# A planner's price of TensorE: a lower rate per column and a larger fixed part

## The chip, the cores and the metric

The kernel runs on one core of a Trainium2 chip. The metric is the device time of one execution, in microseconds (us), median over runs. A core has TensorE (PE: matmuls and transposes), VectorE (DVE), ScalarE (ACT), GpSimd (POOL) and SyncE (SP, whose queue issues all loads and stores here). Each engine takes its own instructions in the order in which the program issued them.

## What is computed

Two layers over a sequence of 512 rows of 1024 float32 values. Each layer:

```
h = rms_norm(x) * g_pre_mix
pool values | q | k | v | indexer q, k, head weights = h @ w_in           # 1024 x 2632
score  = sum over 8 heads of iw * relu(iq . ik / 8)      # 512 x 512, causal by chunks of 64
keys of a row = the 128 largest scores                   # top-k
B = softmax(q . k / 8 over those keys) @ v               # 8 heads of 64
A = averages over windows of 2, 4, 8, 16 rows, minus the row, @ w_pool, * pool_scale
x = x + rms_norm(concat(A, B) @ w_out) * g_post_mix
x = x + rms_norm(relu(rms_norm(x) * g_pre_ffn @ w_ff1)^2 @ w_ff2) * g_post_ffn   # 4096 wide
```

## The kernel before

The 512 rows are four tiles t of 128 rows; a contraction over 1024 is eight chunks kc of 128. Float32 values are split into two float32r parts (a rounded one and the rest), and each product is three matmuls (`mm3`) into one PSUM bank. `A` in SBUF holds the two parts of the normalized rows, transposed.

**Weights** (`WeightStream`) come in chunks of 128 rows by 512 columns (584 for the indexer), 400 in all. SP loads two chunks into a tile `wraw`, of which there are two; `_split` (L445) then writes a tile `ws` from a ring of eight: a cast (`copy`, L536: ScalarE or VectorE) and a subtraction (`tt`, L531: VectorE or GpSimd). `ws.done()` starts the next split when a chunk was last used.

**Stages of a layer.** Indexer projection for t = 0 to 3 (tiles `pi`, 292 columns), with ropes, transposes (`tr`), 8 logits per tile (`lg`), relu and the sum `sc`; then the projections q, k, v (tiles `pg`, 512 columns). `select(t)` (L806) finds the 128 largest scores of a row: 16 rounds on VectorE of MAX8 (`m8`) and MATCH_REPLACE8 (`bias`). `attention(t)` (L871), in the order 2, 3, 0, 1, makes per head logits (`s`), exponentials, a scaling, transposes (`pt`, split into `pT`) and products with v (`po`). The pooling mixer (tiles `pool`, `mx`, `dh`) stands behind attention(2) in the program. The output projection takes tiles 2 and 3, then 0 and 1; each ends in `post_norm` (L686) and `pre_norm`, which scales `h` and transposes it (`hT`) into `A`. The feed-forward network runs in four groups of two blocks of w_ff1 (`pf`, `pg`; relu `fr`, square, split into `f`) and 1024 rows of w_ff2, summed in SBUF (`facc`).

**The planner decides the order.** The program's calls are not issued at once. `_Recorder` (L348) notes each with its price, and `Planner.record` finds what it depends on. `Planner.issue` (L191) makes a list schedule: `sweep` (L227) goes forward through time and gives each engine, of the instructions it could start, the one that must start soonest, then goes backward to find how late each may end (`late`, L222); of 40 such rounds, each with the times of the one before, the shortest is issued. Where an instruction has two possible engines, `sooner` (L258) decides whether one should leave it to the other:

```python
in_time, other = mine <= late[i] - self.SPARE, done <= late[i] - self.SPARE
if in_time and w != 0:
    continue
if other and v != 0 and not (in_time and w != 0):
    return True
```

SPARE is 4000 ns (L95): an instruction that the second engine (v != 0) would end 4 us before its latest time goes there; otherwise it goes where it ends sooner. The second engine is VectorE for casts and relus, GpSimd for subtractions and additions in SBUF, ScalarE for scalings. Prices are in `cost` (L356), waits between engines in LATENCY (L87). A price under 60 ns on TensorE counts as short, and a longer instruction behind a short one starts 54 ns later in the plan (L313 to L315).

Of the kernel before, what the change touches and what calls it, by code (L numbers as in the profile page):

```python
# [18 lines left out]
P = 128  # L19
# [62 lines left out]
class Planner:  # L82
    """Takes the instructions down in program order, finds what each depends on from the tiles that it
    reads and writes, and issues them in the order of a list schedule over the engines: of the
    instructions that an engine could start, the one with the longest chain of work behind it."""
# [55 lines left out]
    def either(self, *ways):  # L141
        """One instruction that several engines can take: each way makes one call."""
        self.collected = []
        for way in ways:
            way()
        found, self.collected = self.collected, None
        self.record([(e, c, f) for e, c, f, _, _ in found], found[0][3], found[0][4])
# [43 lines left out]
    def issue(self):  # L191
        """Sweeps forward and backward over the program in turn, each sweep taking its order of
        preference from the times of the one before, and issues in the order of the best. The first
        order is that of the longest chains behind, with a little noise to part equal ones."""
# [32 lines left out]
    def sweep(self, key, pred, succ, late, fixed=None):  # L227
        """A list schedule. With ``fixed``, the ways are given and time runs backward."""
# [29 lines left out]
        def sooner(t, i, w):  # L258
            """Whether another engine should take instruction i."""
# [76 lines left out]
class _Recorder:  # L336
# [19 lines left out]
    def cost(self, method, args, kw, out, reads):  # L356
        def free(ap):
            return math.prod(c for _, c in list(ap.ap)[1:])
# [6 lines left out]
        if self.name == "pe":  # L365
            if method == "transpose":
                return 56 if args[1].dtype == F32R else 109
            return max(n / 2.4 + 2.5, 107 if free(args[1]) > 64 else 56)
# [16 lines left out]
class WeightStream:  # L385
    """Chunks of weights in the order of their use: loaded, split into two float32r parts, and held
    in a ring until their last use."""
# [21 lines left out]
    def add_paired(self, src, r0, nrows, c0, ncols):  # L409
        """Chunks of 256 rows: rows r and r + 128 side by side."""  # L410
# [59 lines left out]
def hymba_trunk(ctx: ExitStack, tc: tile.TileContext, x, positions, g_pre_mix, w_in, w_pool,  # L470
# [60 lines left out]
    def tt(out, a, b, op, first="dve"):  # L531
        """an elementwise instruction on SBUF, on VectorE or GpSimd"""
        ways = [lambda: dve.tensor_tensor(out, a, b, op=op), lambda: pool.tensor_tensor(out, a, b, op=op)]
        planner.either(*(ways if first == "dve" else ways[:1]))

    def copy(out, a):  # L536
        """a copy, on ScalarE or VectorE"""
        planner.either(lambda: act.activation(out, a, AF.Copy), lambda: dve.tensor_copy(out, a))

    def scaled(out, a, by):  # L540
        """rows times a scalar of each, on VectorE or ScalarE"""
# [109 lines left out]
    def square(out, a, total):  # L651
        """total = the sum of (a / 32) ** 2 along the row: a half's part of the row's mean square"""
        act.activation(out, a, AF.Square, scale=1.0 / 32.0, accum_out=total)

    def rstd_of(parts):
        """parts: [P, 2], the two halves' parts of the row's mean square"""
# [5 lines left out]
    def pre_norm(t, gain):  # L662
        """A[:, :, :, tile t] = the two parts of (RMSNorm(x[t]) * gain) transposed."""
# [22 lines left out]
    def post_norm(t, halves, gain, in_sbuf=False):  # L686
        """x[t] += RMSNorm(halves) * gain"""
# [21 lines left out]
    def rope(row, t, heads):  # L709
        """in place on the first 16 of each head's 64 columns."""  # L710
# [8 lines left out]
    def heads_stacked(dst_hl, row, heads):  # L719
        """dst[128, heads, 2, 64]: the two parts of each head side by side."""  # L720
# [4 lines left out]
    def heads_doubled(dst, row, heads):  # L725
        """dst[128, 2, heads, 2, 64]: either part of each head, twice side by side."""
# [4 lines left out]
    def transposed(dst, srcs):  # L731
        """dst [128, n, 128] <- transposes of n blocks of [128, 128] in float32r."""
# [14 lines left out]
    for l in range(DEPTH):  # L747
# [11 lines left out]
        # indexer projection, logits and scores  # L759
# [103 lines left out]
        # attention  # L863
# [118 lines left out]
        # feed-forward  # L982
# [102 lines left out]
```

## Time and profile before

| | |
|---|---|
| time, median of 3 runs | 1223.35 us (1222.40, 1223.35, 1226.63) |
| profiled execution: first to last instruction (span); its own time beside it is not given | 1222.7 us |
| instructions | 16265, of them 5880 matmuls |
| busy: TensorE, VectorE, GpSimd, ScalarE | 1178.5, 777.1, 668.5, 358.5 us |
| mean granted clock of TensorE | 0.996 |
| read from HBM | 112.27 MB; 94 GB/s over the span with what is written |

"Busy" is the time in which an engine had an instruction under way. What ended an engine's idle time stands in brackets behind the instruction that followed, with the idle time. Stretches are in us from the span's start: attention of layer 0 60 to 240, its output projection and handover to the feed-forward network 240 to 276.9, feed-forward to 605, handover to layer 1 605 to 632, its attention 660 to 840, its feed-forward from 879.5, last matmuls 1207.8 to 1213.5.

### The profile page before, as it was taken

What the parts mean: (1) busy time and instruction counts of PE and PEld (TensorE: products, weight loads), DVE (VectorE), ACT (ScalarE), POOL (GpSimd) and SP (SyncE); (2) the same over time, 40 slices, a digit from 0 to 9 for tenths busy, and PEclk for the clock granted to TensorE, in tenths of its full rate; (3) what the DMA queues carried; (4) which work ended last, traced back from release to release, by engine and by line L of the source; (5) the groups of instructions that cost most, each with busy time, mean ns of one, the idle gap of its engine ahead of it and who ended that gap; (6) DMA issues with size and microseconds to landing.
All of it is one profiled execution on the core that took longest, in us unless ns stands there. A gap on an engine that the chain in (4) does not pass through costs nothing.

```text
span 1222.7 us, 16265 instructions
## 1 busy us (share of the span) xinstructions
PE 1178.5 (96%) x5880; PEld 978.3 (80%) x5880; DVE 777.1 (64%) x1620; ACT 358.5 (29%) x840; POOL 668.5 (55%) x628
## 2 busy tenths in 40 slices
PE   5999999999999999999989999999999999999996
PEld 5987878788888888888887878787888888888885
DVE  8899999875216335245779999998632353343344
ACT  5444677540010000000354367675201000000011
POOL 4145331358659659558334543314785695684782
PEclk9999999999999999999999999999999999999999
DMA  7222222433332322332322222234234223323221
GB/s 242 70 56 67 69 69 88 138 105 121 106 101 69 121 86 71 119 93 90 113 70 69 69 69 69 71 104 138 86 104 121 87 83 107 104 86 104 87 87 69
DMA packets 62160, 115.41 MB, mean 94 GB/s; under 512 B 5248, under 2 KB 10368, under 8 KB 62080
## 3 DMA queue, kind: packets, MB, share of 16 engines
q1 hardware_dynamic: 62080, 114.38, 29.9%
q8 instruction: 46, 0.75, 0.3%
q14 instruction: 34, 0.28, 0.1%
HBM read 112.27 MB, written 2.10 MB: 94 GB/s over the span
## 4 chain that ended last, share of the span: by engine, by line
PE 68%; DVE 23%; issue 5%; POOL 1%; DMA 1%; ACT 0%; DVEq 0%; SPq 0%; POOLq 0%; ACTq 0%
PE pg L349 58%; DVE ws L349 4%; DVE bias L349 3%; PE pi L349 2%; DVE m L349 2%; PE pf L349 2%; DVE mx L349 2%; DVE sc L349 2%; DVE x L349 1%; DVE s L349 1%; DVE A L349 1%; DVE h L349 1%; DVE pT L349 1%; PE lg L349 1%; PE pool L349 1%
## 5 line engine op out<-in xcount | busy, mean ns | idle before, releaser
L349 POOL TENSOR_TENSOR ws<-wraw,ws 128x512 fp32r<-128x512 f32 x296 | 397.6, 1350 | 278.0 <-DVE ws L349 233.3
L349 DVE CAST ws<-wraw 128x512 fp32r<-128x512 f32 (+1 forms) x317 | 195.3, 624 | 337.1 <-PE pg L349 247.4
L349 PE MATMUL pg<-A,ws 128*128 128x512 f32 x1344 | 313.9, 395 | 0.0
L349 PEld LDWEIGHTS pg<-A,ws 128*128 128x128 f32 x1344 | 252.3, 188 | 60.0
L349 PE MATMUL pg<-ws,A 128*128 128x512 f32 x864 | 226.3, 400 | 1.9 <-DVE pn L349 1.6
L349 PE MATMUL pg<-ws,f 128*128 128x512 f32 x768 | 187.0, 394 | 0.0
L349 PEld LDWEIGHTS pg<-ws,A 128*128 128x128 f32 x864 | 156.9, 188 | 33.5 <-DVE pn L349 2.5
L349 PEld LDWEIGHTS pg<-ws,f 128*128 128x128 f32 x768 | 144.1, 188 | 33.6
L349 ACT ACTIVATE fr<-pg 128x512 f32<-128x512 f32 x49 | 27.9, 598 | 475.9 <-PE pg L349 475.1
L349 PE MATMUL pg<-ws,f1h 128*128 128x512 f32 x512 | 149.5, 394 | 0.0
L349 PEld LDWEIGHTS pg<-ws,f1h 128*128 128x128 f32 x512 | 96.1, 188 | 22.5
L349 POOL TENSOR_TENSOR rstd<-rstd,neg_half 128x1 f32<-128x1 f32 x32 | 25.9, 809 | 119.5 <-DVE rstd L349 114.9
L349 PE MATMUL pg<-ws,f1l 128*128 128x512 f32 x256 | 89.1, 393 | 0.0
L349 DVE TENSOR_TENSOR ws<-wraw,ws 128x512 fp32r<-128x512 f32 (+1 forms) x104 | 79.0, 772 | 0.9 <-ACT ws L349 0.5
L349 POOL TENSOR_TENSOR fr<-fr 128x512 f32<-128x512 f32 (+1 forms) x70 | 71.3, 1033 | 12.8 <-ACT fr L349 11.8
L349 ACT ACTIVATE s<-s,st 128x384 f32<-128x384 f32 (+3 forms) x96 | 54.0, 568 | 36.0 <-DVE st L349 32.5
L349 PE MATMUL pi<-ws,A 128*128 128x292 f32 x384 | 60.7, 305 | 2.2 <-DVE ws L349 1.8
L349 ACT ACTIVATE ws<-wraw 128x512 fp32r<-128x512 f32 (+1 forms) x83 | 51.9, 632 | 30.1 <-PE pg L349 19.8
L349 PE MATMUL pool<-A,ws 128*128 128x512 f32 x192 | 58.7, 407 | 0.0
L349 PEld LDWEIGHTS pg<-ws,f1l 128*128 128x128 f32 x256 | 48.1, 188 | 11.2
L349 PEld LDWEIGHTS pi<-ws,A 128*128 128x128 f32 x384 | 53.4, 190 | 3.7 <-DVE ws L349 2.4
L349 DVE CAST f1h<-fr 128x512 fp32r<-128x512 f32 (+1 forms) x40 | 39.2, 997 | 19.0 <-POOL fr L349 19.0
(154 smaller groups left out, 1493.7 us busy)
## 6 DMA issues: line engine op xcount, KB each, us to landing
wraw<-in_w_ff_dram SPq DMA_DIRECT2D x128, 512.0 KB, 3.7
wraw<-in_w_out_dram SPq DMA_DIRECT2D x32, 512.0 KB, 3.6
wraw<-in_w_in_dram SPq DMA_DIRECT2D x24, 512.0 KB, 3.6
wraw<-in_w_in_dram SPq DMA_DIRECT2D x8, 584.0 KB, 4.1
wraw<-in_w_in_dram SPq DMA_DIRECT2D x16, 256.0 KB, 3.0
x<-in_x_dram SPq DMA_DIRECT2D x4, 512.0 KB, 6.3
out_dram<-x SPq DMA_DIRECT2D x8, 256.0 KB, 2.0
gain<-in_g_pre_mix_dram SPq DMA_DIRECT2D x2, 512.0 KB, 4.7
```

The source lines that it names most:

```text
L349: lambda: getattr(self.real, method)(*args, **kw))
```

## The change

`cost` prices TensorE's instructions by other numbers. Nothing else of the program differs, beside comments and docstrings, which issue nothing.

```diff
         if self.name == "pe":
             if method == "transpose":
-                return 56 if args[1].dtype == F32R else 109
-            return max(n / 2.4 + 2.5, 107 if free(args[1]) > 64 else 56)
+                return 59 if args[1].dtype == F32R else 109
+            return max(4.5 + n / 2.25, 111 if free(args[1]) > 64 else 60)
```

In ns, by columns: 512 from 215.8 to 232.1; 384 from 162.5 to 175.2; 292 from 124.2 to 134.3; 256 from 109.2 to 118.3; 128 from 107 to 111; a float32r transpose from 56 to 59, still short. Weights of 64 columns or fewer do not occur. TensorE's large matmuls become 7 to 8% dearer in the plan; all other prices stay. The same work is issued in another order, and some instructions that two engines can take go to the other one.

**VectorE, layer 0, the first weights of q** (`ws_257` to `ws_261`, while the indexer's second tile `irow_201` is roped and split into `ihl`; `bias0` is the selection of tile 0). Before:

```order
L349 CAST ws_257<-wraw_127 128x512
L349 SCALAR_TENSOR_TENSOR bias0_374<-sc0_182,bias0_374 128x128
L349 CAST ihl_204<-irow_201 128x8x64
L349 TENSOR_TENSOR ws_257<-wraw_127,ws_257 128x512
L349 TENSOR_TENSOR ihl_204<-irow_201,ihl_204 128x8x64
L349 TENSOR_TENSOR ws_258<-wraw_127,ws_258 128x512
L349 TENSOR_TENSOR ws_260<-wraw_130,ws_260 128x512
L349 COPY iqS_206<-tr_208 128x512
L349 TENSOR_SCALAR bias0_374<-bias0_374 128x128
L349 CAST ws_261<-wraw_130 128x512
L349 TENSOR_TENSOR ws_261<-wraw_130,ws_261 128x512
```

Now:

```order
L349 CAST ws_257<-wraw_127 128x512
L349 SCALAR_TENSOR_TENSOR bias0_374<-sc0_182,bias0_374 128x128
L349 CAST ihl_204<-irow_201 128x8x64
L349 CAST ws_258<-wraw_127 128x512
L349 TENSOR_TENSOR ihl_204<-irow_201,ihl_204 128x8x64
L349 TENSOR_TENSOR ikh_205<-irow_201,ikh_205 128x128
L349 CAST ws_260<-wraw_130 128x512
L349 TENSOR_SCALAR bias0_374<-bias0_374 128x128
L349 COPY iqS_206<-tr_208 128x512
L349 CAST ws_261<-wraw_130 128x512
```

The four subtractions of `ws_257` to `ws_261` have left VectorE for GpSimd, and the casts of `ws_258` and `ws_260` have come to it from ScalarE; so it goes on for the weights of q, k, v, pool and the first output pass.

**VectorE, layer 1, scores of tile 3** (`sc3_1141`, summed over the heads' relus) beside the selection of tile 2 (`bias2_1216`, `m82_1217`). Before:

```order
L349 TENSOR_SCALAR sc3_1141<-relu_1143,iw_1133 128x512
L349 MAX m82_1217<-bias2_1216 128x8
L349 SCALAR_TENSOR_TENSOR sc3_1141<-relu_1145,iw_1133,sc3_1141 128x512
L349 MATCH_REPLACE bias2_1216<-m82_1217,bias2_1216 128x384
L349 SCALAR_TENSOR_TENSOR sc3_1141<-relu_1147,iw_1133,sc3_1141 128x512
L349 MAX m82_1217<-bias2_1216 128x8
L349 SCALAR_TENSOR_TENSOR sc3_1141<-relu_1149,iw_1133,sc3_1141 128x512
L349 MATCH_REPLACE bias2_1216<-m82_1217,bias2_1216 128x384
L349 SCALAR_TENSOR_TENSOR sc3_1141<-relu_1151,iw_1133,sc3_1141 128x512
```

Now:

```order
L349 TENSOR_SCALAR sc3_1141<-relu_1143,iw_1133 128x512
L349 TENSOR_SCALAR relu_1145<-lg_1144 128x512
L349 MAX m82_1217<-bias2_1216 128x8
L349 SCALAR_TENSOR_TENSOR sc3_1141<-relu_1145,iw_1133,sc3_1141 128x512
L349 MATCH_REPLACE bias2_1216<-m82_1217,bias2_1216 128x384
L349 TENSOR_SCALAR relu_1147<-lg_1146 128x512
L349 MAX m82_1217<-bias2_1216 128x8
L349 SCALAR_TENSOR_TENSOR sc3_1141<-relu_1147,iw_1133,sc3_1141 128x512
L349 MATCH_REPLACE bias2_1216<-m82_1217,bias2_1216 128x384
L349 MATCH_REPLACE bias1_1235<-m81_1236,bias1_1235 128x256
L349 MAX m82_1217<-bias2_1216 128x8
```

The relus of the logits `lg`, 128x512, have come from ScalarE to stand between the sums.

**VectorE, the last instructions of the program** (`post_norm` of tiles 1 to 3; `pg_1843` and `pg_1844` are the last PSUM banks of tiles 2 and 3). Before:

```order
L349 SCALAR_TENSOR_TENSOR x1_112<-pn_1848,rstd_1850,x1_112 128x512 x2
L349 TENSOR_TENSOR facc_1601<-pg_1843,facc_1601 128x512
L349 TENSOR_TENSOR pn_1854<-facc_1601,gain_1549 128x512
L349 TENSOR_TENSOR pn_1851<-facc_1601,gain_1549 128x512
L349 SCALAR_TENSOR_TENSOR rstd_1853<-ss2_1852 128x1
L349 TENSOR_TENSOR facc_1601<-pg_1844,facc_1601 128x512
L349 SCALAR_TENSOR_TENSOR x2_113<-pn_1851,rstd_1853,x2_113 128x512 x2
L349 SCALAR_TENSOR_TENSOR rstd_1856<-ss2_1855 128x1
L349 SCALAR_TENSOR_TENSOR x3_114<-pn_1854,rstd_1856,x3_114 128x512 x2
```

Now:

```order
L349 TENSOR_TENSOR pn_1851<-facc_1601,gain_1549 128x512
L349 SCALAR_TENSOR_TENSOR x1_112<-pn_1848,rstd_1850,x1_112 128x512
L349 SCALAR_TENSOR_TENSOR rstd_1853<-ss2_1852 128x1
L349 TENSOR_TENSOR pn_1854<-facc_1601,gain_1549 128x512
L349 SCALAR_TENSOR_TENSOR x2_113<-pn_1851,rstd_1853,x2_113 128x512
L349 TENSOR_TENSOR facc_1601<-pg_1844,facc_1601 128x512
L349 SCALAR_TENSOR_TENSOR x2_113<-pn_1851,rstd_1853,x2_113 128x512
L349 TENSOR_TENSOR pn_1854<-facc_1601,gain_1549 128x512
L349 SCALAR_TENSOR_TENSOR rstd_1856<-ss2_1855 128x1
L349 SCALAR_TENSOR_TENSOR x3_114<-pn_1854,rstd_1856,x3_114 128x512 x2
```

The accumulation of `pg_1844` has one update of `x2` and one gain product `pn_1854` ahead of it and one of each behind; the second product came from GpSimd.

## Rows read from the trace of the kernel before

**Rows 1.** the page's first part: busy us, share of the span, instructions

```profile
PE 1178.5 (96%) x5880; PEld 978.3 (80%) x5880; DVE 777.1 (64%) x1620; ACT 358.5 (29%) x840; POOL 668.5 (55%) x628
```

**Rows 2.** busy time by stretch: length, busy us and instructions, granted clock, DMA

```profile
330.00:600.00 270.00, 270.00 (x1165) 218.33 (x1164) 114.59 (x155) 18.94 (x37) 177.99 (x138) 1.00 0.30 95
60.00:240.00 180.00, 175.16 (x933) 143.71 (x932) 173.12 (x458) 107.62 (x260) 66.68 (x77) 1.00 0.25 77
660.00:840.00 180.00, 173.87 (x920) 144.09 (x919) 173.17 (x459) 108.94 (x260) 65.35 (x75) 0.99 0.26 79
240.00:276.90 36.90, 34.41 (x251) 31.80 (x250) 29.14 (x53) 17.82 (x43) 18.37 (x21) 1.00 0.35 114
605.00:632.00 27.00, 23.49 (x161) 21.73 (x160) 24.05 (x39) 16.06 (x40) 15.08 (x14) 1.00 0.40 123
```

**Rows 3.** chain that ended last: start us, length us, instructions

```profile
38.08 5.29 PE pi L349 x39
...
276.89 328.79 PE pg L349 x1416
```

**Rows 4.** groups of VectorE, 60:240, then 660:840: busy us, mean ns | idle before

```profile
L349 DVE TENSOR_TENSOR ws<-wraw,ws 128x512 fp32r<-128x512 f32 x27 | 19.8, 738 | 0.1
L349 DVE CAST ws<-wraw 128x512 fp32r<-128x512 f32 x26 | 12.0, 463 | 2.6 <-DMA wraw<-in_w_out_dram 2.4
...
L349 DVE SCALAR_TENSOR_TENSOR sc<-relu,iw,sc 128x512 f32<-128x512 f32 x7 | 7.4, 1062 | 0.0
...
L349 DVE TENSOR_TENSOR mx<-mx 128x512 f32<-128x512 f32 x4 | 3.5, 878 | 0.0
...
L349 DVE TENSOR_SCALAR s<-s,st 128x512 f32<-128x512 f32 x4 | 1.9, 476 | 0.0
...
L349 DVE TENSOR_TENSOR ws<-wraw,ws 128x512 fp32r<-128x512 f32 x28 | 21.3, 765 | 0.1
L349 DVE CAST ws<-wraw 128x512 fp32r<-128x512 f32 x23 | 11.8, 513 | 2.2 <-PE pg L349 1.9 <-DMA wraw<-in_w_out_dram 0.2
```

**Rows 5.** groups of VectorE in the feed-forward stage, 330:600

```profile
L349 DVE CAST ws<-wraw 128x512 fp32r<-128x512 f32 x93 | 62.4, 676 | 137.0 <-PE pg L349 123.6 <-DMA wraw<-in_w_ff_dram 11.4 <-POOL ws L349 1.7
...
L349 DVE TENSOR_SCALAR fr<-pg 128x512 f32<-128x512 f32 x3 | 2.1, 687 | 3.7 <-PE pg L349 3.7
```

**Rows 6.** timeline, start us and length us: VectorE, GpSimd, VectorE

```profile
115.86 1.47 DVE L349 TENSOR_TENSOR ws<-wraw,ws 128x512 fp32r<-128x512 f32 x1
...
115.50 1.29 POOL L349 TENSOR_TENSOR ws<-wraw,ws 128x512 fp32r<-128x512 f32 x1 [1.50 <-ACT ws L349]
...
732.48 0.68 DVE L349 TENSOR_TENSOR ws<-wraw,ws 128x512 fp32r<-128x512 f32 x1
```

**Rows 7.** groups of GpSimd, 60:240

```profile
L349 POOL TENSOR_TENSOR ws<-wraw,ws 128x512 fp32r<-128x512 f32 x28 | 41.0, 1475 | 41.9 <-DVE ws L349 23.2 <-ACT ws L349 12.1 <-PE pt L349 3.6
```

**Rows 8.** timeline of the handover to layer 1: TensorE, then VectorE

```profile
622.01 1.13 PE L349 MATMUL hT<-identf,h 128*128 128x128 f32 x8 [2.57 <-DVE rstd L349]
...
610.69 1.93 DVE L349 CAST ws<-wraw 128x584 fp32r<-128x584 f32 x2
...
617.54 2.38 DVE L349 TENSOR_TENSOR h<-x,gain 128x512 f32<-128x512 f32 x2
```

**Rows 9.** timeline of the end: TensorE, VectorE, GpSimd

```profile
1207.78 5.74 PE L349 MATMUL pg<-ws,f 128*128 128x512 f32 x24
...
1214.56 0.68 DVE L349 TENSOR_TENSOR facc<-pg,facc 128x512 f32<-128x512 f32 x1
1215.30 2.42 DVE L349 SCALAR_TENSOR_TENSOR x<-pn,rstd,x 128x512 f32<-128x512 f32 x2
...
1218.44 1.41 DVE L349 SCALAR_TENSOR_TENSOR x<-pn,rstd,x 128x512 f32<-128x512 f32 x2 [0.66 <-POOL rstd L349]
...
1215.40 1.76 POOL L349 TENSOR_TENSOR pn<-facc,gain 128x512 f32<-128x512 f32 x1
```

**Rows 10.** the start: a load's issue on SP's queue; the chain's first load

```profile
12.78 0.47 SPq L349 DMA_DIRECT2D x<-in_x_dram  x1
...
1.65 5.71 DMA gain<-in_g_pre_mix_dram
```

## The prediction, made before the changed kernel was run

> **What bounds the kernel now.** I read the page's first part, then the chain of waits, then the busy times by stage, then the costliest groups of the two attention stages, and at last the timeline at the places where TensorE stands still. TensorE is busy 1178.5 us [rows 1] of a span of 1222.7, so at most 44 us could ever be won by order alone. In the feed-forward stages it never waits: 270.00 us busy of 270 [rows 2], while VectorE has 115 us of work there and GpSimd 178; whatever the schedule does there is covered by TensorE. The waits lie elsewhere: before the first matmuls, in the two attention stages (4.8 us of 180 and 6.1 us of 180), in the two output projections and handovers (2.5 us of 36.9, 3.5 us of 27) [rows 2], and after the last matmul. In the attention stages VectorE is the second bound: busy 173.1 and 173.2 us of 180, so only 6.9 and 6.8 us are free [rows 2]. TensorE runs a fixed order there, so a late VectorE result becomes a TensorE wait at once.
>
> **How true the two prices are.** On the chain, 1416 matmuls of 512 columns took 328.79 us, 232.2 ns each; 39 of 292 columns took 5.29 us, 135.6 ns [rows 3]. The formula of before gives 215.8 and 124.2, the new one 232.1 and 134.3. So the new price is within 1% of the pace that the trace shows, and the old one was 7 to 8% too low. The granted clock was 1.00 in all these stages [rows 2].
>
> The Trainium skill, page "TensorE: Matmul & The Clock Gate", section "Wait — 56ns, not 53.3ns?", states the pace of warm back-to-back matmuls as the columns over 2.4 GHz plus about 2.5 ns, 215.7 ns at 512 columns. That is the old formula and speaks against this change. By that rule the new plan would make TensorE 16 ns too slow per large matmul, would trust in some 12 us per attention stage (7% of its 175) that aren't there, and the sum below would be up to 24 us worse. The trace does not agree (232.2 ns at a granted clock of 1.00), so the sum goes by the row.
>
> **What a dearer TensorE changes in the plan.** Instructions with two possible engines go to the second one wherever it ends 4 us (SPARE) before its latest time; a slower TensorE makes latest times later. The order shows this. No instruction is added or removed. In the attention stage and output projection of layer 0 (weights of q, k, v, pool and both output passes) 27 more casts of weights stand on VectorE (30 before, 57 now) instead of ScalarE, and 25 subtractions leave VectorE for GpSimd (35 before, 10 now). In layer 1 it is 24 casts (32, now 56) and 18 subtractions (32, now 14). ScalarE is relieved by about 30 us over both layers, but it is busy only 358.5 us of the span [rows 1], so that is worth nothing.
>
> **VectorE's casts and subtractions, layer 0.** A subtraction on VectorE costs 738 ns, a cast 463 ns [rows 4]. A cast is slower where GpSimd is busier: 676 ns in the feed-forward stage [rows 5], where GpSimd is busy 178.0 of 270 us, 66%, against 66.7 of 180, 37%, here [rows 2]. The same shows in single instructions: a subtraction on VectorE that began at 115.86 under a subtraction on GpSimd from 115.50 took 1.47 us, another one 0.68 [rows 6]. With 25 more GpSimd subtractions of 1475 ns [rows 7], 36.9 us, GpSimd comes to 103.6 us, 58%. Between the two rows a cast then costs 463 + (58-37)/(66-37) x 213 = about 615 ns. The 26 casts of the row become 53: 32.6 us in place of 12.0, +20.6. The subtractions give back 25 x 738 = 18.5. Net +2 us.
>
> **Layer 1.** GpSimd goes from 65.4 us [rows 2] to 65.4 + 18 x 1.475 [rows 7] = 92.0 us, 51%. A cast, 513 ns now [rows 4], comes to about 593 by the same way, and 23 of them become 47: 47 x 0.593 - 11.8 = +16.1; the subtractions give 18 x 765 = 13.8 [rows 4]. Net +2 us.
>
> **The other moves in these stages.** Twelve relus of 128x512 go from ScalarE to VectorE, 5 in layer 0 and 7 in layer 1. VectorE had none of that shape; the nearest row, the same operation from PSUM, took 687 ns [rows 5]: +3.4 and +4.8 us. Eight scalings of 128x512 leave VectorE (3 and 5, at 476 ns in layer 0 [rows 4]; I use that for both): -1.4 and -2.4. Seven additions of the pooling mixer leave it (4 and 3, at 878 ns [rows 4]): -3.5 and -2.6. Small copies, ropes and casts come to about +1 each, an estimate from the same rows. The score updates of 128x512 took 1062 ns in layer 0 [rows 4] where a two-input instruction of that size that nothing held took 680 [rows 6]; this excess, 7 x 0.38 = 2.7 us, and its like should grow with GpSimd's share: I put +3 and +1 for that. Together VectorE's load rises by 2 + 3.4 - 1.4 - 3.5 + 1 + 3 = about 4.5 us in layer 0 and 2 + 4.8 - 2.4 - 2.6 + 1 + 1 = about 4 us in layer 1. The free 6.9 and 6.8 us can take all of it (lower bound 0, or a gain of a few us where an order is luckier), or none of it, as the relus and casts stand early, between the scores and the selection, and VectorE is wanted soonest there (upper bound the whole 8.5 us, doubled where a late tile meets another). I take 7 of the 8.5: the nearest rows are those of a VectorE with 4% to spare that has no empty stretch early on. **+7 us.**
>
> **The handover to layer 1.** TensorE waited 2.57 us at 622.01 for the transposes of tile 2, whose rows VectorE scales last before them [rows 8]. Between the accumulation of tile 2 and that scaling two casts of 128x584 (1.93 us) and one of two gain products (half of 2.38) [rows 8], with one subtraction (0.74 as rows 4), go to other engines in the new order, 3.9 us in all; into their place come a gain product, two subtractions for A and the scaling of tile 1, some 2.6 us at 0.68 or less for each [rows 9]. Three more matmuls of 292 columns also stand ahead of the transposes on TensorE, 0.4 us [rows 3]. That is -1.3 - 0.4 = -1.7; bounds 0 and -2.6. I take **-1 us**, since the other half of the gain product now runs on GpSimd, beside VectorE's, and holds it.
>
> **The end.** The last 24 matmuls end at 1213.52. The accumulation started at 1214.56, since two gain products stood ahead of it, then two updates of x took 2.42 us under a gain product on GpSimd of 1.76 us, and the square root came behind [rows 9]. Now that product is VectorE's (0.68 us, as the accumulation), only one update stands behind the accumulation, and one ahead of it. Counted from 1213.7, when the last sums are there: accumulation 0.68, update 0.7, product 0.68, which ends at 1215.8; from there the chain is as it is now from 1217.72, the end of the updates, to 1219.85, that of the last one [rows 9]: 2.13 us, to 1217.9. I take **-1.4 us**, as the update ahead may end late; bounds -1.9 and 0.
>
> **The start.** The load of x1 goes ahead of the first weights, and the loads of x2 and x3 ahead of the third weights, which x3 had waited behind until 12.78 [rows 10]. The first projection matmuls may come later, since their weights wait for one more load: the first gain took 5.71 us from issue to landing beside three others [rows 10], a quarter of that is 1.4 us. The later waits for x2 and x3 may shrink by as much or a little more. Bounds -2 and +1.5; I put **0**.
>
> Sum: +7 - 1 - 1.4 = +4.6 us on the profiled span of 1222.7, so 1227.3. Nothing is shown of the time around the span; the median of the three runs is 1223.35, 0.65 above it. With that the forecast is **1228.0 us**, 0.4% slower.
>
> **The rivals.**
> *Faster, the plan fits.* TensorE's planned times are now those of the chip, so its order holds what is ready. The waits of rows 2 are 4.8 + 6.1 + 2.5 + 3.5 = 16.9 us; if half goes, -8.5, and with the end -1.4: 1213.5 us. For it speak rows 3. Against it: the engine that ends these waits is VectorE, whose price, without the holds by GpSimd, is as it was. It decides where a cast in the attention stage of layer 0 stays under (19.8 + 12.0) / 53 = 0.60 us [rows 4]: below that VectorE has no more weight work than before. Chance 0.30.
> *No change.* The free 6.9 and 6.8 us take up the new load, and the gains at the handover and the end are set against small losses: 1221 to 1226 us, 1224 as its middle. For it: TensorE has filler matmuls of q, k, v and pool for most of these stages. Chance 0.28.
> *GpSimd is late.* It does the ropes of q and k between the subtractions, in a fixed order. Each rope that meets a subtraction ahead of it waits some 1.4 us [rows 7], and the transposes of that tile on TensorE with it; with 8 such chains over both layers this adds 11 us to the forecast: 1239 us. For it: GpSimd at 58%. Against it: 42% of its time is still free, and the ropes' due times were planned. Chance 0.10.
> *The change does nothing.* Excluded, since the order moves 51 casts and 43 subtractions in the two stages alone.
>
> **How the numbers follow.** The forecast has 0.32. A measurement of this kernel can tell about 0.3%, 3.7 us, from no change. Slower by more: 0.32 + 0.10 = 0.42; within: 0.28; faster: 0.30. The range goes from the faster rival's 1213 to a little above the late GpSimd's 1239, 1241 us; the forecast's own range, by the lower bounds of its terms (0, -2.6, -1.9, -2) and the upper ones (8.5, 0, 0, 1.5), is 1217 to 1233, and 1242 with the 8.5 doubled.
>
> **What would show it.** The casts of weights on VectorE should be some 368 in the page's groups (317 now), the GpSimd subtractions some 347 (296), GpSimd's busy time about 70 us up and ScalarE's about 35 us down. Right, if the cast takes about 615 ns in the attention stage of layer 0, VectorE's idle time there falls below 4 us and TensorE's waits rise by some 3 us in each such stage. Wrong, if the cast stays near 463 ns, or TensorE's waits fall while VectorE is as full as before, or if the difference lies at the start.

## The result, and the profile after

The changed kernel took **1272.79 us** (median of 4 runs, 1270.68 to 1276.15) against 1223.99 us before (4 runs beside it): ratio 1.0399, 95% interval 1.0378 to 1.042. That is slower, as forecast, but by 48.8 us and not by 4.6, and far outside the range of 1213 to 1241. The profiled execution took 1270.68 us with a span of 1268.9.

The page's first part of the changed kernel, to be read against [rows 1]:

```profile
PE 1196.6 (94%) x5880; PEld 988.1 (78%) x5880; DVE 789.9 (62%) x1626; ACT 324.2 (26%) x775; POOL 743.8 (59%) x687
```

The span grew by 46.2 us. TensorE is busy 18.1 us longer with the same 5880 matmuls, and stands idle 72.3 us in place of 44.2. The moves of work are those of the order: GpSimd is 75 us busier, ScalarE 34 us less.

The changed kernel by the stretches of [rows 2], in the same order but for the first, which is last here:

```profile
60.00:240.00 180.00, 165.35 (x865) 134.32 (x866) 171.69 (x449) 83.57 (x205) 84.15 (x91) 0.98 0.23 68
660.00:840.00 180.00, 165.97 (x885) 138.31 (x883) 167.99 (x430) 78.19 (x188) 89.92 (x96) 0.95 0.21 62
240.00:276.90 36.90, 34.26 (x178) 27.96 (x176) 32.33 (x59) 21.77 (x54) 12.02 (x12) 1.00 0.40 121
605.00:632.00 27.00, 26.92 (x121) 21.68 (x120) 16.86 (x28) 7.66 (x18) 11.51 (x11) 1.00 0.26 82
330.00:600.00 270.00, 269.59 (x1161) 217.25 (x1160) 104.98 (x143) 15.79 (x28) 188.58 (x147) 1.00 0.31 95
```

The feed-forward stage is covered by TensorE as before. In the two long stretches TensorE's idle time rose from 4.8 to 14.7 us and from 6.1 to 14.0 us, and its granted clock fell from 1.00 and 0.99 to 0.98 and 0.95. VectorE's busy time in these fixed windows fell, 173.1 to 171.7 and 173.2 to 168.0 us, but the slower kernel has done less of the layer's work by their end.

These stretches hide where the time went. Cut at the last matmul of the indexer projection (`pi`) and at the first attention logits (`s`), in whole us, each layer has a selection stage (projections q, k, v on TensorE beside the selection on VectorE) and an attention stage. Before, then the changed kernel, layer 0 and layer 1, in the columns of [rows 2]:

```profile
51.00:118.00 67.00, 66.21 (x325) 53.99 (x325) 66.86 (x162) 30.12 (x58) 31.59 (x48) 1.00 0.22 63
118.00:225.00 107.00, 102.46 (x585) 84.60 (x584) 103.56 (x298) 73.50 (x192) 30.68 (x29) 1.00 0.25 80
650.00:718.00 68.00, 64.17 (x316) 52.37 (x316) 67.69 (x169) 31.43 (x61) 34.78 (x50) 1.00 0.24 70
718.00:827.00 109.00, 105.29 (x593) 88.32 (x592) 104.31 (x293) 73.88 (x191) 30.93 (x27) 0.98 0.24 78
```

```profile
53.00:130.00 77.00, 68.90 (x323) 55.48 (x323) 75.79 (x174) 20.38 (x37) 37.80 (x53) 0.96 0.19 56
130.00:245.00 115.00, 105.27 (x588) 85.70 (x587) 107.67 (x298) 67.29 (x180) 53.87 (x46) 1.00 0.24 74
676.00:758.00 82.00, 72.67 (x324) 58.81 (x323) 80.03 (x187) 18.70 (x36) 48.11 (x61) 0.90 0.25 71
758.00:867.00 109.00, 102.88 (x581) 84.21 (x580) 97.95 (x283) 68.86 (x180) 45.77 (x40) 1.00 0.21 68
```

By TensorE's timeline the selection stages grew by 9.6 and 13.6 us, half of the loss; the attention stages by 8.5 and 1.4, the indexer projections by 2.1 and 2.2, the output projections by 2.2 and 3.9, the handover and all the rest by 2.7. In the selection stage VectorE had nothing to give before, 66.86 of 67 us, and has almost nothing now, 75.79 of 77. Over both stages its busy time rose by 13.0 us in layer 0 (66.86 + 103.56 to 75.79 + 107.67) and by 6.0 us in layer 1 (67.69 + 104.31 to 80.03 + 97.95).

What TensorE waits for, from the list of its waits (us in total, times, longest), before and after:

```profile
PE tr L349 <- DVE ihl L349: 3.6, 2, 3.0
PE s L349 <- DVE st L349: 2.8, 6, 0.8
```

```profile
PE tr L349 <- DVE ihl L349: 9.1, 4, 3.8
PE s L349 <- DVE st L349: 6.9, 7, 2.7
PE tr L349 <- DVE khl L349: 5.2, 2, 2.6
PE tr L349 <- DVE kS L349: 3.4, 2, 3.2
```

The longest are for transposes of the indexer's rows (`ihl`) and of k (`khl`): TensorE arrives at them in its fixed order and VectorE has not written the rows yet. For `kS` the transposes wait until VectorE has copied earlier ones out of PSUM. One such place, the first transposes of `khl` in layer 0, on TensorE's timeline (start us, length us), before and after:

```profile
86.87 17.80 PE L349 MATMUL pg<-ws,A 128*128 128x512 f32 x76
104.50 0.79 PE L349 MATMUL tr<-ident,khl 128*128 128x128 f32 x8
```

```profile
95.87 15.68 PE L349 MATMUL pg<-ws,A 128*128 128x512 f32 x67
114.15 0.88 PE L349 MATMUL tr<-ident,khl 128*128 128x128 f32 x8 [2.60 <-DVE khl L349]
```

And VectorE in the changed kernel, the score update beside which that stretch begins, another one, and the write that ends the wait:

```profile
95.42 1.53 DVE L349 SCALAR_TENSOR_TENSOR sc<-relu,iw,sc 128x512 f32<-128x512 f32 x1
...
99.39 0.73 DVE L349 SCALAR_TENSOR_TENSOR sc<-relu,iw,sc 128x512 f32<-128x512 f32 x1
...
113.42 0.68 DVE L349 TENSOR_TENSOR khl<-krow,khl 128x512 fp32r<-128x512 f32 x1
```

Here the mechanism can be counted. The old plan put 76 matmuls of projections ahead of these transposes, the new one 67: at 216 ns a matmul the plan needs 76 to fill 16.4 us, at 232 ns 67 to fill 15.6. VectorE's 32 instructions from 95.42 to the end at 114.10 cost 15.07 us by the prices of L373 to L376, so the new plan sees cover enough. They took 18.68 us. TensorE's 67 took 15.68, almost exactly as priced. The right price for TensorE met a price for VectorE that is a fifth too low here, and TensorE waited 2.60 us. In the plan of before 25 of VectorE's instructions stood at this place, 13.3 us by the same prices; they took 14.1 us and were done 3.2 us before the transposes began. Of the 3.6 us by which the new plan's 32 overran, 1.6 are two score updates of 1.53 us, each beside a subtraction of weights on GpSimd, where a third took 0.73. So a part of the overrun is not a wrong rate but GpSimd holding VectorE (last section).

How far VectorE's prices are off shows in its groups of the selection stage before (busy us, mean ns):

```profile
L349 DVE MAX8 m<-bias 128x8 f32<-128x384 f32 x15 | 8.2, 543 | 0.0
L349 DVE MATCH_REPLACE8 bias<-m,bias 128x384 f32<-128x384 f32 x15 | 8.0, 536 | 0.0
L349 DVE SCALAR_TENSOR_TENSOR sc<-relu,iw,sc 128x512 f32<-128x512 f32 x7 | 7.4, 1062 | 0.0
...
L349 DVE MATCH_VALUE_LOAD bias<-m,bias 128x8 f32 x33 | 2.5, 75 | 0.0
```

The plan prices the first two at 469 ns each and the load of 75 ns that goes with the second at nothing, the score update at 662, a cast of 512 columns at 336 ([rows 4]: 463 and 513), a subtraction at 602 ([rows 4]: 738 and 765). TensorE's old price was 7% too low as well [rows 3]. The two errors leaned against each other: that is the explanation which the experiments below test.

### The profile page after: what moved, and what is told of

It reads as the page before. It is cut to its first block, busy times and chain, and to the rows that moved or that the text cites. A ratio compares the mean times of both kernels' runs of the same rounds, so it can differ in the third digit from the quotient of the medians.

```text
span 1268.9 us, 16236 instructions
## 1 busy us (share of the span) xinstructions
PE 1196.6 (94%) x5880; PEld 988.1 (78%) x5880; DVE 789.9 (62%) x1626; ACT 324.2 (26%) x775; POOL 743.8 (59%) x687
## 4 chain that ended last, share of the span: by engine, by line
PE 61%; DVE 29%; issue 4%; POOL 2%; ACT 2%; DMA 2%; DVEq 0%; POOLq 0%; SPq 0%; ACTq 0%
PE pg L349 53%; DVE ws L349 5%; DVE bias L349 4%; DVE m L349 3%; PE pf L349 2%; DVE s L349 2%; DVE sc L349 2%; DVE x L349 2%; DVE h L349 2%; PE pi L349 1%; DVE A L349 1%; DVE mx L349 1%; DVE pT L349 1%; PE lg L349 1%; DMA wraw<-in_w_ff_dram 1%
## 5 line engine op out<-in xcount | busy, mean ns | idle before, releaser
L349 POOL TENSOR_TENSOR ws<-wraw,ws 128x512 fp32r<-128x512 f32 (+1 forms) x347 | 463.1, 1341 | 307.5 <-DVE ws L349 269.3
L349 DVE CAST ws<-wraw 128x512 fp32r<-128x512 f32 (+1 forms) x368 | 215.7, 594 | 370.2 <-PE pg L349 254.5
L349 PE MATMUL pg<-ws,A 128*128 128x512 f32 x864 | 234.4, 410 | 3.1 <-DVE pn L349 3.1
L349 PEld LDWEIGHTS pg<-ws,A 128*128 128x128 f32 x864 | 162.0, 194 | 35.8 <-DVE pn L349 4.0
L349 POOL TENSOR_TENSOR fr<-fr 128x512 f32<-128x512 f32 (+1 forms) x72 | 74.9, 1053 | 16.5 <-ACT fr L349 14.5
L349 ACT ACTIVATE s<-s,st 128x384 f32<-128x384 f32 (+3 forms) x106 | 61.0, 583 | 55.9 <-DVE st L349 55.5
L349 POOL TENSOR_TENSOR rstd<-rstd,neg_half 128x1 f32<-128x1 f32 x32 | 21.9, 684 | 68.4 <-DVE rstd L349 68.1
L349 DVE CAST f1h<-fr 128x512 fp32r<-128x512 f32 (+1 forms) x40 | 42.8, 1088 | 16.7 <-POOL fr L349 16.7
L349 PE MATMUL pf<-A,ws 128*128 128x256 f32 x384 | 50.3, 288 | 2.4 <-DVE A L349 2.3
L349 PEld LDWEIGHTS pf<-A,ws 128*128 128x128 f32 x384 | 47.9, 193 | 3.5 <-DVE A L349 2.7
```

The lines of the kernel that those rows point to most:

```text
L349: lambda: getattr(self.real, method)(*args, **kw))
```

## The experiments

Four theories were set against each other. **1, the engines:** the casts and relus put on a full VectorE are the loss. **2, the order:** a dearer TensorE makes a worse order whatever the rest. **3, chance:** any new plan scatters, and the old seed suited the old price. **4, the ratio** (formed after the second set): TensorE alone became dearer, so the plan trusts VectorE with time that it doesn't have, in its order and in its choice of engines. All times are medians; the kernel before took 1224.1 to 1225.2 us beside them.

**Chance: another seed with either price.**

```diff
-    SEED = 53
+    SEED = 1
```

> The new price with another seed of the noise. The order has 16 and 14 casts of the stage on VectorE and 13 relus. Theory 1: as the change, 1260 to 1280. Theory 2: the same. Theory 3, that SEED 53 was a lucky one for the old price alone: about as likely below 1250 as above.

> The old price with the same other seed: 5 and 6 casts of the stage on VectorE, no relu. Theories 1 and 2: close to before, 1220 to 1235. Theory 3: well above before, as the change is, 1240 to 1285, since SEED 53 was picked with the old price.

Measured: 1271.94 us with the new price (ratio 1.0391), 1228.68 with the old (1.0037). Theory 3 falls: the loss stays, the seed moves 1 and 4 us. With the control below this also tells how far two plans of the same prices differ, some 0.4%, from three pairs; smaller differences are given no cause here, and one of 9 or 10 us between single plans is only twice that.

**Engines by SPARE.** More SPARE keeps casts on ScalarE, less sends them to VectorE.

```diff
-    SPARE = 4000.0
+    SPARE = 16000.0        # new price;  2000.0 with the old price
```

> Stage = from the last matmul of the indexer projection to the first attention logits, where VectorE runs the selection. In the order of this kernel, the new price with SPARE at 16000, VectorE has 4 and 4 of that stage's casts of weights (before 2 and 6, the change 16 and 19), and one relu (the change 12). Theory 1, the engines: what costs is the casts and relus put on a full VectorE in that stage, so the time comes back to 1217 to 1235 us and the stage to 68 to 71 us in either layer (before 66.9 and 68.4, the change 76.5 and 82.0). Theory 2, the order itself: TensorE's dearer price makes an order that is worse whichever engine casts; the time stays at 1255 to 1275. Theory 3, chance: any other plan scatters, anywhere from 1220 to 1290.

> The old price with SPARE at 2000: the order has 14 and 14 casts of weights of the stage on VectorE, and 8 relus. Theory 1: slower than before without any change of price, 1245 to 1270 us, the stage 73 to 80 us. Theory 2: the old price's order stays good, 1220 to 1232. Theory 3: anywhere from 1220 to 1290.

Measured: 1256.71 us (1.0266) and 1252.36 (1.0231). With the old price, untouched, another choice of engines, with the order planned for it, loses 28 us, as theory 1 says. With the new price only 16 of 49 us come back, which is inside theory 2's band and outside theory 1's; the stages took 74.7 and 74.6 us and not 68 to 71. SPARE 16000 also leaves 11 and 10 subtractions of the stage on VectorE, so its load is not that of before, and VectorE is again full in the stage (73.89 of 75 us).

**The order kept, the casts moved.** The list MOVED holds the program's numbers of these instructions.

```diff
         self.planned, start, way = best
+        for i in self.MOVED:
+            way[i] = 0          # ScalarE;  1 (VectorE) in the plan of before
```

> The change's own order of instructions, word for word, but the 16 and 19 casts of weights and the 5 and 7 relus that it puts on VectorE between the last projection matmul of the indexer and the first logits run on ScalarE, at the same places of the order. Theory 1, the engines: VectorE is full in that stage (75.8 of 77.0 us, 80.0 of 82.0), so its length falls by what is taken away, 16 x 0.59 + 5 x 0.67 = 12.8 us and 19 x 0.59 + 7 x 0.67 = 15.9 us at most, less where another wait comes up: 9 to 16 us a layer, 1272.8 to 1242 to 1254 us. Theory 2, the order: under 6 us in all, 1266 to 1274.

> The order of before, but its 13 and 11 casts of weights that ScalarE does in the same stage run on VectorE; nothing else moves and no price changes. Theory 1: each lengthens the stage by its own time, 0.46 to 0.6 us, 24 of them by 11 to 14 us, and a little more if TensorE's waits lower its clock: 1235 to 1242 us. Theory 2: VectorE takes them beside TensorE, 1222 to 1229 us.

Measured: 1257.15 us (1.027) and 1233.38 (1.008). Both lie between the bands of theories 1 and 2. The casts back on ScalarE shorten the selection stages by 5.7 and 6.5 us, less than expected; 24 casts moved to VectorE lengthen them by 5.2 and 5.5 us, 0.40 and 0.50 us for each cast. So VectorE's load in the stage is paid nearly in full in the plan of before, but it is a third of the loss. The selection stages of the first of the two:

```profile
53.00:124.00 71.00, 66.70 (x322) 54.34 (x321) 66.61 (x157) 31.74 (x58) 37.80 (x53) 0.98 0.21 60
...
668.00:743.00 75.00, 69.70 (x322) 56.75 (x321) 67.81 (x162) 33.18 (x62) 45.80 (x61) 0.93 0.27 77
```

VectorE now has 4.4 and 7.2 us free, and the stages are still 4 to 7 us longer than before, with TensorE waiting too. What is left is the order, or moves that this run left alone: the subtractions on GpSimd, and all moves outside this stage.

**Engines and order crossed.** Every instruction with two engines is bound to a given one, and the order is planned anew. The list of choices, WAYS, is left out here.

```diff
+        bits = iter(bin(int(self.WAYS, 16))[3:])
+        ops = self.ops = [([o[0][int(next(bits))]], *o[1:]) if len(o[0]) > 1 else o for o in self.ops]
```

> The new price, planned anew, but every instruction that has two engines to choose from goes where before put it; only the order is free. Theory 1: 1218 to 1235 us, the stage 66 to 70 us in either layer. Theory 2, the dearer TensorE spoils the order: 1250 to 1275.

> The old price, planned anew, with every choice of engine as the change made it. Theory 1: 1255 to 1278 us, the stage 74 to 82 us. Theory 2: 1220 to 1240.

> A control for the two runs with engines given: the old price, planned anew with the choices of engine that before made itself. If planning with the engines given costs nothing, 1222 to 1232 us; then the 28 and 32 us of the two mixed runs are the engines' and the order's. If it costs something by itself, 1240 to 1258, and the mixed runs say less.

Measured: 1256.93 us (1.0269, in theory 2's band), 1252.28 (1.0231, between the two but near theory 1's), and the control 1230.53 (1.0048), 5 us above the kernel before, about what two seeds differ by. Counted from the control, the new price costs 26.4 us through the order alone and 21.8 us through the engines alone; the sum, 48.2 us, is about the change's loss. That the two add up is not shown, since the new price bound to the change's own engines wasn't run. Theories 1 and 2 each hold about half. With the change's engines the selection stages took 71.8 and 70.1 us, below theory 1's 74 to 82; 10 of the 22 us lie in layer 1's attention stage. With the engines of before they took 72.7 and 73.6. There TensorE waits 7.2 us in the selection stage of layer 0 (3.5 for ScalarE's and 2.2 for VectorE's part of `khl`, 1.0 for `ihl`, 0.5 for `irow`), in the control 0.8 us.

**The ratio.** All other prices, lags and allowances times 1.075; the scaled lags and allowances are left out here:

```diff
+        return self.price(method, args, kw, out, reads, free, psum) * (1.0 if self.name == "pe" else 1.075)
```

> The new price of TensorE, and every other price, lag and allowance of the plan times 1.075 (what the new formula adds at 512 columns), so that the ratios of before hold again except for the small instructions of TensorE. Theory 4, the ratio: what costs is that TensorE alone became dearer, so that the plan believes VectorE to have 7.5% of time that it doesn't have, in its order and in its choice of engines alike; the ratio of before brings 1222 to 1238 us. Theory 1 alone, the engines (5 and 13 casts of weights in the stage on VectorE, no relus): 1232 to 1250. Theory 2, the right price of TensorE spoils the order whatever the others are: 1250 to 1275.

Measured: 1238.74 us (1.0112), 0.7 above theory 4's band, inside theory 1's and outside theory 2's. 34 of 49 us are back with the same new price of TensorE, so the price by itself isn't the cause. The largest part of the rest, 6.0 of 13.6 us, lies in layer 1's selection stage, with 13 casts of weights on VectorE.

**VectorE's and GpSimd's prices set by the trace.** These are means over stages, so what VectorE and GpSimd cost each other is in them.

```diff
-            return 70 + (0.52 if fast else 1.04) * n + 60 * scalars
+            return 70 + (1.0 if fast else 1.3) * n + 60 * scalars     # VectorE
-            return (70 + 1.2 * n) if method == "tensor_scalar" else (464 if n == 1 else 50 + 2.3 * n)
+            return (70 + 1.2 * n) if method == "tensor_scalar" else (464 if n == 1 else 50 + 2.8 * n)   # GpSimd
```

> The new price, with VectorE's and GpSimd's prices nearer to the trace as well: a VectorE copy at 1.0 ns an element (a cast of 512 columns 582 ns; measured 594), other VectorE instructions 1.3 (736; a subtraction measured 738), GpSimd 2.8 (1484; measured 1475 before). 5 and 6 casts of weights in the stage on VectorE, 4 and 5 subtractions, one relu. Theory 4: TensorE's part is as dear against VectorE as before or less, so the time comes back, 1210 to 1235 us. Theory 2: 1250 to 1275. Theory 1: 1222 to 1236.

> The same dearer VectorE and GpSimd with the old price of TensorE. 1 and 1 casts of weights in the stage on VectorE, 7 and 5 subtractions. Theory 4: VectorE is spared more than before; if sparing it is what counts, 1205 to 1228 us; if the ratio of before was the best one, 1228 to 1245. Theory 2: 1220 to 1230, since TensorE's price is the old one.

Measured: 1222.71 us (0.9988, 0.9975 to 1.000) and 1212.6 (0.9898). The loss is gone with the new price in place, and theory 2 falls; theories 1 and 4 both allow this time. With the old price the same edit beats the kernel before by 1%. That misses the branch of theory 4 by which the ratio of before is the best one, 1228 to 1245.

One at a time with the new price:

> The new price, and VectorE's copies at 1.0 and its other instructions at 1.3 ns an element; GpSimd and the selection as they were. 8 and 8 casts of weights in the stage on VectorE, 0 and 1 subtractions. If VectorE's price is what the low TensorE price was an offset for: 1222 to 1240 us. If GpSimd's counts as much: 1240 to 1262.

> The new price, and GpSimd at 2.8 ns an element; VectorE as it was. 14 and 19 casts of weights in the stage on VectorE. If VectorE's price is what counts: 1260 to 1276 us. If GpSimd's: 1225 to 1250.

Measured: 1229.67 us (1.0046) and 1263.01 (1.0314). VectorE's prices, all but the selection's, give back 43 of 49 us, GpSimd's 10, and both together 50, so they overlap.

**The selection's price.** It has no second engine, so its price can act through the order alone.

```diff
-                return 70 + 1.04 * free(args[-1] if method == "max" else args[2])
+                return (150 if method == "max" else 216) + 1.03 * free(args[-1] if method == "max" else args[2])
```

> The new price, the dearer VectorE and GpSimd of the run before, and the selection's two instructions priced by the trace as well, 150 and 216 ns + 1.03 an element instead of 70 + 1.04 (512 elements: 677 and 743; measured 678, and 669 + 75 for the load that comes with it). 1 and 2 casts of weights in the stage on VectorE. Theory 4, the ratio in order and engines: the selection is the largest part of VectorE's work there, so pricing it rightly gives TensorE's order the filler it lacked, 1205 to 1219 us (1222.7 without it). Theory 5, only prices of instructions with two engines count, since the selection has but one: 1219 to 1228.

> The same with the old price of TensorE. Theory 4 with true ratios best: no better than the run beside it, 1208 to 1222 us, as TensorE is now the one priced too low. If sparing VectorE is good without end: under 1208. Theory 5: 1208 to 1216, as old_price_dearer_others (1212.6).

> The new price with only the selection's two prices set by the trace; 17 and 11 casts of weights in the stage on VectorE still. Theory 4: a part of the loss comes back by the order, 1235 to 1260 us. Theory 5: 1262 to 1276.

Measured: 1212.19 us (0.9889, 0.9868 to 0.9911), 1221.63 (0.9972) and 1263.81 (1.0313). The last is in the band of theory 5, that only instructions with two engines count, and just above theory 4's: alone, the selection's price gives back 9 us at most. The other two speak against theory 5: with VectorE's and GpSimd's other prices by the trace, the selection's price wins 10.5 us beside the new TensorE price and loses 9 beside the old one. So "dearer VectorE is always better" falls as well. With it in place the new price of TensorE is the better by 9.4 us, without it the old one by 10.1. Each of these is one plan, and no other seed was tried. ScalarE's prices stayed as they were in every run, though a cast of 512 columns is priced at 520 ns there and took 627 before. The selection stages and attention stages of new_all_dearer, and the place that was counted above (here 115 matmuls stand ahead of the transposes of `khl`, and nothing waits):

```profile
53.00:118.00 65.00, 64.61 (x320) 52.99 (x319) 60.83 (x142) 34.38 (x67) 36.68 (x54) 1.00 0.28 80
118.00:221.00 103.00, 102.08 (x591) 86.53 (x591) 93.88 (x272) 86.78 (x219) 32.13 (x29) 1.00 0.25 79
645.00:711.00 66.00, 65.73 (x323) 53.49 (x322) 63.02 (x140) 33.23 (x66) 40.58 (x58) 1.00 0.24 70
711.00:814.00 103.00, 101.70 (x587) 85.72 (x587) 94.92 (x273) 82.51 (x214) 36.95 (x33) 1.00 0.25 79
```

```profile
80.16 26.83 PE L349 MATMUL pg<-ws,A 128*128 128x512 f32 x115
106.82 0.81 PE L349 MATMUL tr<-ident,khl 128*128 128x128 f32 x8
```

VectorE has 4 and 9 us free in layer 0, ScalarE has taken 18 us more there than before, and TensorE idles 1.3 us in the two stages together.

**The parts of the new formula.** The old rate, 2.4 columns per ns in place of 2.25, with the new fixed parts (transposes 59, 128 columns 111).

> The old rate per column with the new fixed parts alone: transposes 59 instead of 56, matmuls of 128 columns 111 instead of 107. 8 and 9 casts of weights in the stage on VectorE (before 2 and 6). Theory 4: the rate at 512 columns carries the loss, 1224 to 1240 us. The opposite, the small instructions carry it by the end of the fillers: 1250 to 1275.

Measured: 1238.13 us (1.0103). Inside theory 4's band: with the dearer small instructions alone the plan is 13 us slower. The rate alone wasn't tried.

| TensorE's price | the other prices | us | to before |
|---|---|---|---|
| old | old | 1224 to 1225 | 1 |
| new | old | 1272.8 | 1.0399 |
| new | GpSimd's by the trace | 1263.0 | 1.0314 |
| new | all times 1.075 | 1238.7 | 1.0112 |
| new | VectorE's except the selection's by the trace | 1229.7 | 1.0046 |
| new | these and GpSimd's by the trace | 1222.7 | 0.9988 |
| new | VectorE's and GpSimd's by the trace | **1212.2** | 0.9889 |
| old | the same without the selection's | 1212.6 | 0.9898 |
| old | VectorE's and GpSimd's by the trace | 1221.6 | 0.9972 |

## Why the prediction was wrong

**The pace of TensorE: right.** In the chain of the changed kernel 1414 matmuls of 512 columns took 328.50 us, 232.3 ns each, as in [rows 3]:

```profile
924.36 328.50 PE pg L349 x1414
```

The Trainium skill's 215.7 ns ("TensorE: Matmul & The Clock Gate", "Wait — 56ns, not 53.3ns?") would have made the new plan the worse one for a reason that isn't there; the trace disagrees again. The times of whole plans do not settle which price is truer, since the dearer one is better by 9.4 us beside one set of prices and worse by 10.1 beside another.

**The moves and their prices: right in size for one instruction, too small as a load.** Groups of VectorE and GpSimd, 60:240, and of VectorE, 660:840, to set against [rows 4] and [rows 7]:

```profile
L349 DVE CAST ws<-wraw 128x512 fp32r<-128x512 f32 x45 | 25.7, 580 | 1.2 <-PE pg L349 0.6 <-POOL ws L349 0.6
...
L349 DVE TENSOR_SCALAR relu<-lg 128x512 f32<-128x512 f32 x5 | 3.3, 669 | 0.0
...
L349 POOL TENSOR_TENSOR ws<-wraw,ws 128x512 fp32r<-128x512 f32 x45 | 60.5, 1352 | 54.3 <-DVE ws L349 42.7 <-DVE st L349 3.4 <-PE s L349 2.8
...
L349 DVE CAST ws<-wraw 128x512 fp32r<-128x512 f32 x43 | 23.0, 543 | 2.9 <-PE pi L349 2.4 <-PE pool L349 0.5
```

A cast took 580 and 543 ns where I had 615 and 593, a relu 669 where I had 687. In the page's groups 368 casts stand on VectorE and 347 subtractions on GpSimd, as foretold. But VectorE's busy time over the two stages of a layer rose by 13.0 and 6.0 us, where I had 4.5 and 4. Two of the signs did not come either: VectorE's idle time in 60:240 was to fall below 4 us and rose from 6.9 to 8.3, and TensorE's waits were to rise by some 3 us in each long stretch and rose by 9.9 and 7.9.

**The step that failed: "the free 6.9 and 6.8 us can take all of it ... I take 7 of the 8.5."** It has three faults. First, the 8.5 itself was too small: the load rose by 19 us. Second, I summed over 60:240 and 660:840, where the subtractions that leave VectorE nearly pay for the casts that come. The casts come into the selection stage, where VectorE had 0.1 and 0.3 us free, and most of the subtractions left the attention stage (of 27 and 28 on VectorE before, 6 and 5 stood in the selection stage). Seven us were foreseen for both layers; with the order kept, taking casts and relus back won 15.6 us.

Third, and largest, I treated the load of VectorE as the whole effect, and the order as given. "How true the two prices are" tested TensorE's price alone. In a list schedule a price is only a claim against the other engines' prices, and rows that I had on the table stood 23 to 101% above those (a subtraction at 738 ns against 602, [rows 4]; a cast at 463 to 676 against 336, [rows 4, 5]). With the order alone free, the new price cost 26.4 us, a term that my sum did not have. Nor had it the clock behind the waits (last section).

**The rivals.** "Faster, the plan fits" had its deciding point at a cast under 0.60 us. The cast came to 0.58, and the kernel was 4% slower: the point was worked out from the load and missed the order. Once VectorE's and GpSimd's prices fit too, the new price came to 1212.2 us, near that rival's 1213.5; but the old price came to 1212.6 with part of them, so the number does not prove its mechanism. "GpSimd is late" added 11 us, to 1239, and was far too small. A GpSimd price by the trace gave back 10, but no wait of TensorE in the list of the changed kernel's waits is put down to GpSimd, so that rival's chain isn't shown.

**The handover, forecast -1.** The wait for the transposes of `h` is now 3.22 us at 647.67 in place of 2.57, and the clock was half behind it. Missed.

```profile
647.67 1.06 PE L349 MATMUL hT<-identf,h 128*128 128x128 f32 x8 [3.22 <-DVE h L349]
```

**The end, forecast -1.4.** TensorE ends at 1258.85, and from there to the end of the span it is 10.0 us, 0.9 more than before. Set against [rows 9], the accumulation starts 2.64 us after the last matmul and not 1.04, since a held update of 1.77 us and a chain of a square root and an update stand ahead of it. I had allowed for a late update, but counted from an accumulation that starts at once.

```profile
1255.91 2.94 PE L349 MATMUL pg<-ws,f 128*128 128x512 f32 x12
...
1257.88 1.77 DVE L349 SCALAR_TENSOR_TENSOR x<-pn,rstd,x 128x512 f32<-128x512 f32 x1
...
1261.49 0.68 DVE L349 TENSOR_TENSOR facc<-pg,facc 128x512 f32<-128x512 f32 x1
```

**The start, forecast 0.** The first projection matmul moved from 11.20 to 11.35 us. Right; but the indexer projections behind it grew by 2.1 and 2.2 us, for which the sum had no term.

## What to carry to other kernels

The prices of a list schedule are worth something only against one another: before one is corrected, set each of them beside the trace, and correct them together, or two errors that leaned on each other come apart. A stage in which one engine is full must be read by itself, cut where its work begins and ends. In an engine's fixed order, count the filler ahead of each hand-off, and the time that the other engine really takes for what it has to do meanwhile.

## What was not expected of the hardware

**A wait can cost again in clock.** TensorE's time under way rose by 18.1 us for the same matmuls, 39% of the span's growth. Its mean granted clock fell from 0.996 to 0.986, which over the two spans is 4.9 and 17.8 us of full-speed time; so at most about 13 of the 18.1 us are the clock's, an estimate, and the rest is open. In the run with the new price and the engines of before the clock was 0.982, in its control 0.995: by the same count up to 16 of the 26.4 us put down to the order are clock lost behind its waits. Windows of 2 us in the changed kernel, around a wait of 3.80 us for `ihl` that ended at 60.62 (the granted clock is the third column from the end):

```profile
58.00:60.00 2.00, 0.00 (x0) 0.00 (x0) 2.00 (x3) 0.05 (x1) 2.00 (x2) 1.00 0.59 225
60.00:62.00 2.00, 1.38 (x8) 1.25 (x9) 1.93 (x7) 0.60 (x1) 0.01 (x1) 0.94 0.39 65
62.00:64.00 2.00, 2.00 (x8) 1.50 (x8) 1.86 (x7) 0.38 (x1) 0.00 (x0) 0.50 0.51 198
64.00:66.00 2.00, 2.00 (x10) 1.59 (x9) 1.86 (x7) 0.36 (x1) 0.00 (x0) 0.71 0.00 0
66.00:68.00 2.00, 2.00 (x12) 1.75 (x11) 1.74 (x7) 1.22 (x3) 0.00 (x0) 1.00 0.00 0
```

Half clock, the 1.2 GHz level, began about 1 us after TensorE was at work again and held for some 3 us. The same followed the waits of 3.53, 2.59 and 3.22 us in layer 1's selection stage, where the clock was 0.90 on the whole. A wait is no sure sign: before, one of 3.03 us that ended at 656.04 was followed by 1.00 throughout, and one of 1.92 us at 787.75 by 0.62 and 0.53. What decides between them stays open.

**A hold by GpSimd makes a small instruction as long as a large one.** In the same place VectorE, then GpSimd:

```profile
57.59 1.28 DVE L349 CAST ikh<-irow 128x128 fp32r<-128x128 f32 x1
...
59.13 1.42 DVE L349 TENSOR_TENSOR ihl<-irow,ihl 128x512 fp32r<-128x512 f32 x1
```

```profile
57.27 2.73 POOL L349 TENSOR_TENSOR ws<-wraw,ws 128x512 fp32r<-128x512 f32 x2 [0.36 <-DVE ws L349]
```

The cast of 128 columns took 1.28 us beside two subtractions on GpSimd; with GpSimd idle one took 0.21 before:

```profile
54.62 0.21 DVE L349 CAST ikh<-irow 128x128 fp32r<-128x128 f32 x1
```

The Trainium skill ("SBUF — State Buffer", "Summary: rules for kernel authors") says that where VectorE is in a 2-port mode, or reads two inputs from SBUF while GpSimd's instruction reads SBUF, the second of the two to issue is blocked until the first is done. The rows agree in their lengths; the cast's mode no row shows. A price that depends on an instruction's own size cannot hold that.

These two instructions stand ahead of the transposes that waited 3.80 us, and by the unhindered 0.21 and 0.68 us [rows 6] they lost 1.8 us, an estimate. So holds by GpSimd are a part of the loss. They are not all of it: with SPARE at 16000 GpSimd had 28 and 26 us of work in the selection stages, in place of 38 and 48, and the stages still took 75 us each. No run separates them.
